# All convolution taps of x's first mixer on one engine, and the other stream's last steps moved behind the convolution

## The chip, the cores and the metric

The kernel runs on one core of a Trainium2 chip. A core has five engines with queues of their own: TensorE (PE) multiplies matrices, VectorE (DVE), ScalarE (ACT) and GpSimd (POOL) work elementwise, and SyncE (SP) issues the transfers from memory. The metric is the device time of one launch in microseconds (us). Three runs of the kernel before gave 2197.45, 2197.75 and 2201.2 us, a median of 2197.75.

## The reference

Two stacked networks run on 256 tokens of width 1024. The first (`first_block`) is a recurrent layer, an attention layer and two dense feed-forward layers. The second (`second_block`) takes its output `x` and a second stream `ctx` (here `xc`), also 256 tokens. Its layer 0 passes each stream through the same mixer, and then both streams together through a mixture of 32 experts. The change is in that mixer for `x`, and in where the last part of it for `xc` stands:

```python
def fourier_conv_mixer(h, w_in, conv_w, conv_b, conv_g, w_out):
    p = h @ w_in
    pa, pu, pg = jnp.split(p, [512, 1024], axis=-1)
    ya = jnp.fft.fft2(pa ..., axes=(1, 3), norm='ortho').real
    u = pu * jax.nn.sigmoid(pg)
    u = conv_general_dilated(u, conv_w ...) + conv_b   # depthwise, 31 taps
    yb = jax.nn.silu(rmsnorm(u, conv_g))
    return jnp.concatenate([ya, yb], axis=-1) @ w_out
...
x  = x  + g1  * fourier_conv_mixer(h, *ab)
xc = xc + cg1 * fourier_conv_mixer(hc, *ab)
...
out = hier_moe(concat([h2, hc2]), *moe)    # h2, hc2: normed x, xc
```

The convolution has 31 taps on each of 512 channels. Behind it stand a norm over the 512 channels, a SiLU, and the product with the second half of `w_out`.

## The kernel before

Features lie on the 128 partitions, tokens along the row: x and xc are 8 tiles of 128x256. A product in full precision is three products (high by high, high by low, low by high part; lines 405 to 407), so every weight chunk is first cut into a high part (ACT, line 382, `wh`) and a low part (DVE, line 383, `wl`). A chunk of 1 MB gives two such cuts, and `_K.run` makes them up to four steps ahead of the product that uses them. Products go to PSUM buffers named `mm`, of which there are three. The engine that reads a buffer out frees it for a later product.

The program is a list of steps. `_fourier` writes the mixer once for each stream. For x its steps stand in the main list: the input products (`signal`, `transform_in`), the Fourier part (`transform_rows`, `transform_cols`), the first half of the output product (`out(0, ci)`: four steps of 24 matmuls, two tiles of x each), then `gather` (what is left of the taps, and the squares), `root` (the norm's sum and inverse root), `norm` (per 128 channels a scaling on DVE, the SiLU on ACT, and the two parts), and the second half of the output product (`out(1, ci)`). Behind it come the norm and the routing of x, and the experts, whose weights (`gu`, `down`) are fetched in 1 MB pieces by SP.

For xc the steps go to a list of their own, `K.heavy`. `fill()` is called at 181 places ("spots") of the main list, and at each takes as many steps from `K.heavy` as the digit of the table HEAVY at that spot says. So HEAVY alone decides where xc's steps stand among those of x. `K.light` (the products with `mod_w`, line 1083) is spread by a second table, which does not change.

The taps are queued as closures in `K.later`, one list for DVE and one for POOL, when `signal` has made `u`. `drain` steps then take a few from each list after each product step. A tap on DVE is one instruction (line 417, `cv = u*w + cv`). A tap on POOL is an ACT product into a tile `tap` (line 421) and a POOL sum (line 424). Before the change 16 of 31 taps went to DVE into `cv` and 15 to POOL into a second sum `cg`, which `gather` adds to `cv` (line 1240). For x the three lists of interest around the end of the stage are these, by spot:

| spot | step of x behind it | steps of xc there before | steps of xc there after |
|---|---|---|---|
| 149 | signal(2), second half | out(1,0) first half | none |
| 162 to 164 | out(0, ci) | the other three halves of out(1, ci), freeing and entering of pools, the three steps of the norm before routing | none |
| 166 | root | none | all four halves of out(1, ci) |
| 167 | norm | the two scalings by that norm | pools, first step of the norm before routing |
| 168 | out(1,0) first half | router product, two turns of the tokens, a pool freed | second and third step of that norm |
| 169 | out(1,0) second half | ring of four expert buffers entered | the two scalings |
| 170, 171 | out(1,1) | none | router product and first turn; second turn and a pool freed |
| 172 | end of the mixer | none | ring of four expert buffers entered |

Of the kernel before, what the change touches and what calls it, by code (L numbers as in the profile page):

```python
# [18 lines left out]
P = 128  # L19
D = 1024  # L20
T = 256
# [132 lines left out]
class _K:  # L154
# [258 lines left out]
    def tap(self, eng, out, src, w, new, act=False):  # L413

        nc = self.nc
        if eng is nc.vector:
            eng.scalar_tensor_tensor(out, src, w, out, op0=ALU.mult, op1=ALU.add)
            return
        t = new()[:, :src.shape[1]]
        if act:  # L420
            nc.scalar.activation(t, src, AF.Copy, scale=w)
        else:
            eng.tensor_scalar(t, src, w, 0.0, op0=ALU.mult, op1=ALU.add)
        eng.tensor_tensor(out, out, t, op=ALU.add)

    def drain(self, nv=0, ng=0):

        def fn():
            for q, n in ((self.later[0], nv), (self.later[1], ng)):
                for _ in range(min(n, len(q))):  # L430
                    q.pop(0)()
        self.add(fn)
# [210 lines left out]


WARM = [8, 4, 4, 6]
HEAVY = "0000000000000100000000000000000000010101001000110000000000022001000001000000301000000010000000100001000100000000001000010000000000000000010000131301010000000000008110024100000000000"
LIGHT = "0000001101020010310001000110302000001010100100110100000500000000000000000100000000000000000100100000000000000000000000000000000000000001000011001001110000110000000001020300000000000"


# [502 lines left out]
    return ([first] if summed else [first, second, third]) + [scale(0), scale(4)]  # L1152


def _fourier(K, src, r, pool, to, conv, sums=None):

    nc = K.nc
    mm = nc.tensor.matmul
    B = _Box(K, pool)

    def begin():
        B.new("hh", [P, KC, T], F32R)
        B.new("hl", [P, KC, T], F32R)
        B.new("u", [P, 4, T + 30])
        B.new("cv", [P, 4, T])
        B._t["cg"] = B.new("cg", [P, 4, T]) if conv else B.cv
        B.new("fa", [P, 4, T])
        B.new("taps", [P, 124])
        nc.vector.tensor_scalar_mul(B.taps, K.v("conv_w_2", 0, 124), 0.5)
        nc.gpsimd.memset(B.u[:, :, 0:15], 0.0)  # L1170
        nc.gpsimd.memset(B.u[:, :, T + 15:], 0.0)

    def tap(eng, out, j, k, first):
        def fn():
            w = B.taps[:, k * 4 + j:k * 4 + j + 1]
            win = B.u[:, j, k:k + T]
            if first:
                bias = K.v("conv_b_2", j) if k == 0 else 0.0
                eng.tensor_scalar(out[:, j], win, w, bias, op0=ALU.mult, op1=ALU.add)
            else:  # L1180
                K.tap(eng, out[:, j], win, w, lambda: B.new("tap", [P, T], bufs=2), act=conv > 0)
        return fn

    def signal(j):
        def fn(h, wh, wl):
            ps = K.pt()[:, :T]
            K.lin(ps, wh, wl, B.hh, B.hl)
            if h == 0:
                B.new("sg", [P, T])

                nc.scalar.activation(B.sg, ps, AF.Tanh, scale=0.5)
            else:
                nc.vector.scalar_tensor_tensor(B.u[:, j, 15:15 + T], B.sg, 1.0, ps, op0=ALU.add, op1=ALU.mult)
                for k in range(31):
                    e = k >= conv
                    K.later[e].append(tap((nc.vector, nc.gpsimd)[e], B.cg if e else B.cv, j, k, k in (0, conv)))
        return fn

    def transform_in(ci):
        def fn(h, wh, wl):  # L1200
            ps = K.pt()[:, :T]
            K.lin(ps, wh, wl, B.hh, B.hl)
            nc.scalar.activation(B.fa[:, 2 * ci + h], ps, AF.Copy)
        return fn

    def transform_rows(g):
        def fn():
            if g == 0:
                B.new("ch", [P, KC, T], F32R, tag="hh")
                B.new("cl", [P, KC, T], F32R, tag="hl")  # L1210
            ps = K.pt()
            for t in range(2):
                mm(ps[:, t * 256:t * 256 + 256], lhsT=B.fa[:, g, t * P:t * P + P], rhs=K.dft[:, 0:256],
                   start=True, stop=True)
            B.new(f"ab{g}", [P, 2, 2, P], tag="ab", bufs=2)
            nc.scalar.activation(B._t[f"ab{g}"].rearrange("p t c j -> p (t c j)"), ps, AF.Copy)
        return fn

    def transform_cols(g):
        def fn():  # L1220
            ps = K.pt()[:, :T]
            ab = B._t[f"ab{g}"]
            for t in range(2):
                for c in range(2):
                    mm(ps, lhsT=ab[:, t, c], rhs=K.dft[:, 256 + c * 512 + t * 256:512 + c * 512 + t * 256],
                       start=t + c == 0, stop=t + c == 2)
            K.parts(B.ch[:, g], B.cl[:, g], ps)
        return fn

    rms = _Rms(K, lambda: B.cv, 4, RMS_EPS)  # L1230
    done = _Rms(K, src, KC, RMS_EPS, "acc")

    def gather():
        for q in K.later:
            while q:
                q.pop(0)()
        for q in range(2):
            if conv:
                qs = slice(2 * q, 2 * q + 2)
                nc.vector.tensor_add(B.cv[:, qs], B.cv[:, qs], B.cg[:, qs])  # L1240
            rms.square(q)

    def root():
        rms.add(0)
        rms.add(1)
        rms.root()

    def norm():
        rs = rms.row()
        for j in range(4):  # L1250
            nc.vector.scalar_tensor_tensor(B.cv[:, j], B.cv[:, j], K.v("conv_norm_g_2", j), rs,  # L1251
                                           op0=ALU.mult, op1=ALU.mult)
            nc.scalar.activation(B.cv[:, j], B.cv[:, j], AF.Silu)
            K.parts(B.ch[:, 4 + j], B.cl[:, 4 + j], B.cv[:, j])

    def out(part, ci):
        def fn(h, wh, wl):
            for i in range(2):
                m = 4 * ci + 2 * h + i
                c = slice(i * P, i * P + P)  # L1260
                ps = K.pt()[:, :T]
                K.lin3(ps, lambda k: wh[:, k, c], lambda k: wl[:, k, c], lambda k: B.ch[:, 4 * part + k],
                       lambda k: B.cl[:, 4 * part + k], 4)
                nc.vector.scalar_tensor_tensor(src[:, m], ps, K.mod[0][:, r, 16 + m:17 + m], src[:, m],
                                               op0=ALU.mult, op1=ALU.add)
            if part == 1 and conv:
                q = 2 * ci + h
                done.square(q)
                if q > 0:
                    done.add(q - 1)  # L1270
        return fn

    def drain(n=1):
        if to is None:
            K.drain(5 * n, 3 * n)

    def weights(*args, **kw):
        n = len(K.steps)
        K.addw(*args, to=to, **kw)
        if to is None:  # L1280
            last = K.steps.pop()
            drain()
            K.fill()
            K.steps.append(last)
            drain()

    K.add(begin, to)
    def here():
        if to is None:
            K.fill()  # L1290
    for fn in _modulate(K, src, 0, r, 0, K.v("norm_mix_g_2", 0, 8), pool, parts=lambda: (B.hh, B.hl), rms=sums):
        K.add(fn, to)
        here()
    for j in range(4):
        weights("w_in_ab_2", j, signal(j))
        here()
    for ci in range(2):
        weights("w_in_ab_2", 4 + ci, transform_in(ci))
        here()
    for g in range(5):  # L1300
        if g < 4:
            K.add(transform_rows(g), to)
        if g > 0:
            K.add(transform_cols(g - 1), to)
        drain()
        here()
    for ci in range(2):
        weights("w_out_ab_2", ci, out(0, ci), kind=(4, 256))
        here()
    for fn in (gather, root, norm):  # L1310
        K.add(fn, to)
        here()
    for ci in range(2):
        weights("w_out_ab_2", 2 + ci, out(1, ci), kind=(4, 256))
        here()
    if conv:
        K.add(lambda: done.add(KC // 2 - 1))
    return done

# [945 lines left out]
def _kernel(ctx, tc, a):  # L2265
    K = _K(ctx, tc, a)
# [2 lines left out]
    K.add(lambda: K.enter("big"))  # L2269
    for l in range(DEPTH):  # L2270
        _modulation(K, l, K.light)
    _fourier(K, K.xc, 1, "cx", K.heavy, 0)
    moe = _Moe(K, 0, [(K.xc, 1), (K.x, 0)])
    K.add(lambda: K.leave("cx"), K.heavy)
    K.add(moe.enter, K.heavy)
# [4 lines left out]
    sums = _first_block(K, X)  # L2280
    K.add(lambda: K.leave("big"))
    K.add(lambda: K.enter("mx"))
    rms = _fourier(K, K.x, 0, "mx", None, 16, sums)
    K.flush(K.heavy)
    K.flush(K.light)
    K.add(lambda: K.leave("mx"))
# [11 lines left out]
    sums = moe.rms  # L2298
    moe = later
    rms = _attention(K, sums)  # L2300
# [23 lines left out]
```

## Time and profile before

| | |
|---|---|
| profiled execution | 2197.75 us, of which the span is 2196.0 us |
| PE busy | 1937.6 us, 88% of the span |
| DVE busy | 1128.7 us, 51% |
| ACT busy | 812.6 us, 37% |
| POOL busy | 422.9 us, 19% |
| x's first mixer, from the first `u` to the sum of the last norm's squares | 823.25 to 958.05 us of the span |
| first expert product | 983.74 us |

The page's shares are means over the whole span, and the change touches 135 us of it. It is read from windows of the span, which give each engine's busy time and PE's granted clock in one stretch, and from the timeline, where a row is one instruction or a run of equal ones: start, time from the first's start to the last's end, engine, line, operation, output and inputs, shapes, count, and in brackets the idle time before it and what ended it. Matmuls whose operands are plain f32 are recorded as two passes each (lines 564, 1083, 1225, 1727, 1738 among them), so that their counts are twice those of the program; those of lines 405 to 407 are recorded once.

### The profile page before, as it was taken

To read this page: it belongs to the slowest core of one execution; us is meant where nothing else is said; L and a number is where in the kernel's file an instruction comes from. 1 tells how busy PE (TensorE), PEld (TensorE's weight loads), DVE (VectorE), ACT (ScalarE), POOL (GpSimd) and SP (SyncE) were. 2 spreads that over 40 slices of the span, in tenths; PEclk is the share of its full clock that TensorE was granted. 3 is DMA by queue.
4 is the path that set the end of the run, shared out by engine and by line. 5 is a ranking of instruction groups with operands and counts; after the bars stand their busy time and mean duration, and the time that the engine had idled before them with its cause. 6 is when DMAs were issued, how large, how long until landed. Compare 5 with 4: busy or idle time off the path is not lost. (4 is left out here: it accounts for less than half of the span.)

```text
span 2196.0 us, 34689 instructions
## 1 busy us (share of the span) xinstructions
PE 1937.6 (88%) x13286; PEld 1336.9 (61%) x13292; DVE 1128.7 (51%) x2081; ACT 812.6 (37%) x1430; POOL 422.9 (19%) x470
## 2 busy tenths in 40 slices
PE   6889999999979998788999898997999897787876
PEld 6769997988979977663444444434877442233332
DVE  7665673666847568753443443445554332222333
ACT  5544653554546446432222222224454221111221
POOL 5122430799952106300000000001000000000000
PEclk9999999999989999899999899998999999988998
DMA  6477655543444544368999699992224899999995
GB/s 240 175 300 267 235 214 224 219 147 142 155 152 173 192 173 173 137 267 333 419 418 419 259 396 418 419 408 77 99 77 180 323 417 418 419 418 418 419 418 218
DMA packets 86428, 602.65 MB, mean 274 GB/s; under 512 B 9632, under 2 KB 12064, under 8 KB 13856
## 3 DMA queue, kind: packets, MB, share of 16 engines
q1 hardware_dynamic: 86176, 599.24, 68.8%
q8 instruction: 164, 2.69, 0.5%
q14 instruction: 88, 0.72, 0.1%
HBM read 598.15 MB, written 1.05 MB: 273 GB/s over the span
## 5 line engine op out<-in xcount | busy, mean ns | idle before, releaser
L405 PE MATMUL mm<-xh,wh 128*128 128x256 f32 x1024 | 294.0, 287 | 12.2 <-ACT wh L382 11.4
L407 PE MATMUL mm<-xh,wl 128*128 128x256 f32 x1024 | 292.0, 285 | 5.8 <-DVE wl L383 4.8
L406 PE MATMUL mm<-xl,wh 128*128 128x256 f32 x1024 | 292.1, 285 | 0.6 <-DVE xl L480 0.3
L1972 PE MATMUL acc<-down,hT 128*64 128x512 f32 x1024 | 263.3, 623 | 7.6 <-PEq L2124 2.7
L1915 DVE TENSOR_TENSOR gs<-gs,acc 64x512 f32<-64x512 f32 x81 | 55.2, 682 | 316.4 <-ACT gs L1914 316.4
L405 PEld LDWEIGHTS mm<-xh,wh 128*128 128x128 f32 x1024 | 198.0, 193 | 21.8 <-ACT wh L382 12.3
L407 PEld LDWEIGHTS mm<-xh,wl 128*128 128x128 f32 x1024 | 197.9, 193 | 7.0 <-DVE wl L383 5.7
L406 PEld LDWEIGHTS mm<-xl,wh 128*128 128x128 f32 x1024 | 198.2, 194 | 1.8 <-DVE xl L480 1.6
L1908 PE MATMUL acc<-gu,xc 128*32 128x512 f32 x1120 | 145.1, 629 | 57.5 <-DMA gu<-in_gu_dram 47.0
L1908 PE MATMUL acc<-gu,xg 128*32 128x512 f32 x1472 | 174.3, 610 | 13.2 <-PEq L2146 6.5
L1972 PEld LDWEIGHTS acc<-down,hT 128*64 128x64 f32 x1024 | 87.8, 142 | 160.4 <-issue 143.4
L1965 DVE SCALAR_TENSOR_TENSOR yl<-acc,wsl,yh 128x512 fp32r<-128x512 f32 x64 | 48.1, 751 | 200.7 <-ACT yh L1964 186.3
L1914 ACT ACTIVATE gs<-acc 64x512 f32<-64x512 f32 x81 | 48.0, 593 | 260.7 <-PE acc L1908 259.0
L383 DVE TENSOR_TENSOR wl<-ffn_w_up,wh 128x1024 fp32r<-128x1024 f32 x96 | 126.4, 1329 | 27.0 <-ACT wh L382 26.8
L405 PE MATMUL mm<-hh,wh 128*128 128x256 f32 (+1 forms) x416 | 129.1, 310 | 6.5 <-DVE cv L1251 3.5
L1964 ACT ACTIVATE yh<-acc,wsl 128x512 fp32r<-128x512 f32 x64 | 44.0, 687 | 221.8 <-PE acc L1972 221.8
L406 PE MATMUL mm<-hl,wh 128*128 128x256 f32 (+1 forms) x416 | 124.5, 299 | 0.6 <-DVE hl L397 0.3
L407 PE MATMUL mm<-hh,wl 128*128 128x256 f32 (+1 forms) x416 | 124.0, 298 | 0.4 <-DVE wl L383 0.3
L882 DVE SCALAR_TENSOR_TENSOR hv<-mm,vec,hv 128x255 f32<-128x255 f32 x192 | 88.2, 480 | 64.1 <-ACT hv L877 60.2
L920 PE MATMUL acc<-gl,wh 128*128 128x256 f32 x384 | 109.6, 285 | 11.5 <-POOL gl L905 11.5
L1908 PEld LDWEIGHTS acc<-gu,xg 128*32 128x32 f32 x1472 | 51.3, 111 | 110.3 <-issue 88.7
L382 ACT ACTIVATE wh<-ffn_w_up 128x1024 fp32r<-128x1024 f32 x96 | 101.0, 1056 | 40.5 <-PE mm L406 17.1
(501 smaller groups left out, 4343.9 us busy)
## 6 DMA issues: line engine op xcount, KB each, us to landing
gu<-in_gu_dram SPq DMA_DIRECT2D x256, 1024.0 KB, 19.8
down<-in_down_dram SPq DMA_DIRECT2D x128, 1024.0 KB, 19.8
mod_w<-in_mod_w_dram SPq DMA_DIRECT2D x48, 1024.0 KB, 4.9
ffn_w_up<-in_ffn_w_up_dram SPq DMA_DIRECT2D x48, 1024.0 KB, 4.8
ffn_w_down<-in_ffn_w_down_dram SPq DMA_DIRECT2D x24, 1024.0 KB, 4.8
w_in_ab<-in_w_in_ab_dram SPq DMA_DIRECT2D x12, 1024.0 KB, 4.8
kv_w<-in_kv_w_dram SPq DMA_DIRECT2D x8, 1024.0 KB, 7.2
w_out_ab<-in_w_out_ab_dram SPq DMA_DIRECT2D x8, 1024.0 KB, 4.8
```

The lines of the kernel that those rows point to most:

```text
L382: nc.scalar.activation(wh, src, AF.Copy)
L383: self.lows.append(lambda: nc.vector.tensor_sub(wl, src, wh))
L405: mm(out, lhsT=wh(k), rhs=xh(k), start=s, stop=False, **kw)
L406: mm(out, lhsT=wh(k), rhs=xl(k), start=False, stop=False, **kw)
L407: mm(out, lhsT=wl(k), rhs=xh(k), start=False, stop=e, **kw)
L882: nc.vector.scalar_tensor_tensor(hv[:, s, d:], ps[:, s * T:(s + 1) * T - d], cw(2 - d, m), hv[:, s, d:], op0=ALU.mult, op1=ALU.add)
L920: mm(ps, lhsT=wh[:, k], rhs=gl[:, k], start=False, stop=False, skip_group_check=True)
L1908: mm(gu[quarters[g]], lhsT=xk(2 * j + k), rhs=w[:, k, h], start=j == 0, stop=j == 3, tile_position=(0, LOT * g), skip_group_check=True)
L1914: nc.scalar.activation(gs[to], gu[other], AF.Copy)
L1915: nc.vector.tensor_tensor(gs[to], gs[to], gu[to], op=ALU.add)
L1965: nc.vector.scalar_tensor_tensor(yl, ps, wsl, yh, op0=ALU.mult, op1=ALU.subtract)
L1972: mm(ys[n][64 * s:64 * s + 64], lhsT=hT[:, at(c)], rhs=part(ws[s], c)[:, n * 512:n * 512 + 512], start=c == 0, stop=c == 3, tile_position= ...
```

## The change

All 31 taps of x go to DVE into the one sum `cv`; the second sum, its addition and x's POOL and ACT tap instructions go. A drain takes five taps, six where it stands behind a Fourier step (`drain(6)`). `to is None` takes the place of `conv` as the sign of x. xc's taps stay on POOL. In HEAVY the last 18 steps of xc move as the table above shows.

```diff
-HEAVY = "0000000000000100000000000000000000010101001000110000000000022001000001000000301000000010000000100001000100000000001000010000000000000000010000131301010000000000008110024100000000000"
+HEAVY = "0000000000000100000000000000000000010101001000110000000000022001000001000000301000000010000000100001000100000000001000010000000000000000010000131301000000000000000000452222100000000"
...
-def _fourier(K, src, r, pool, to, conv, sums=None):
+def _fourier(K, src, r, pool, to, eng, sums=None):
...
-        B._t["cg"] = B.new("cg", [P, 4, T]) if conv else B.cv
...
-                K.tap(eng, out[:, j], win, w, lambda: B.new("tap", [P, T], bufs=2), act=conv > 0)
+                K.tap(eng, out[:, j], win, w, lambda: B.new("tap", [P, T], bufs=2))
...
                 for k in range(31):
-                    e = k >= conv
-                    K.later[e].append(tap((nc.vector, nc.gpsimd)[e], B.cg if e else B.cv, j, k, k in (0, conv)))
+                    K.later[eng is nc.gpsimd].append(tap(eng, B.cv, j, k, k == 0))
...
         for q in range(2):
-            if conv:
-                qs = slice(2 * q, 2 * q + 2)
-                nc.vector.tensor_add(B.cv[:, qs], B.cv[:, qs], B.cg[:, qs])
             rms.square(q)
...
-    def drain(n=1):
+    def drain(n=5):
         if to is None:
-            K.drain(5 * n, 3 * n)
+            K.drain(n)
...
-        drain()
+        drain(6)
...
-    _fourier(K, K.xc, 1, "cx", K.heavy, 0)
+    _fourier(K, K.xc, 1, "cx", K.heavy, K.nc.gpsimd)
...
-    rms = _fourier(K, K.x, 0, "mx", None, 16, sums)
+    rms = _fourier(K, K.x, 0, "mx", None, K.nc.vector, sums)
```

DVE's queue at the end of the taps. In the kernel before, from the last cuts ahead of `gather` to the norm: `xc<-mm` and `x<-mm` are the sums of output tiles into the streams, `cv<-cv,cg` is the addition of the two sums:

```order
L1264 SCALAR_TENSOR_TENSOR xc<-mm,mod_1090,xc 128x256 x2
L1116 SCALAR_TENSOR_TENSOR msc<-mod_1090,vec 128x8
L383 TENSOR_TENSOR wl<-w_out_ab_9630,wh 128x1024
L1264 SCALAR_TENSOR_TENSOR x<-mm,mod_1090,x 128x256 x2
L383 TENSOR_TENSOR wl<-w_out_ab_9630,wh 128x1024
L1264 SCALAR_TENSOR_TENSOR x<-mm,mod_1090,x 128x256 x2
L447 TENSOR_SCALAR ra<-mm 128x2
```

and in the changed kernel, the same place:

```order
L1259 SCALAR_TENSOR_TENSOR x<-mm,mod_1090,x 128x256 x2
L417 SCALAR_TENSOR_TENSOR cv<-u,taps,cv 128x256 x24
L383 TENSOR_TENSOR wl<-w_out_ab_9281,wh 128x1024
L1259 SCALAR_TENSOR_TENSOR xc<-mm,mod_1090,xc 128x256 x2
L383 TENSOR_TENSOR wl<-w_out_ab_9515,wh 128x1024
L1259 SCALAR_TENSOR_TENSOR xc<-mm,mod_1090,xc 128x256 x2
L383 TENSOR_TENSOR wl<-w_out_ab_9515,wh 128x1024
L1259 SCALAR_TENSOR_TENSOR xc<-mm,mod_1090,xc 128x256 x4
L447 TENSOR_SCALAR ra<-mm 128x2
```

Twenty-four taps now stand in one piece, and all eight sums of xc's tiles come behind them, ahead of the root (`ra`).

PE's queue from the sum of the convolution's squares (line 564, `mm<-sq,ones`) to the second half of x's output product. Before (`mm<-rd,ones` spreads an inverse root over the partitions, `mm<-rw,h2T` is xc's router product, `cst,h2T` its turns):

```order
L564 MATMUL mm<-sq,ones 32x256 x4
L574 MATMUL mm<-sel,tot 128x1 x2
L586 MATMUL mm<-rd,ones 128x256
L1083 MATMUL mod<-mod_w_9437,sc 32x512 x4
L1083 MATMUL mod<-mod_w_9587,sc 32x512 x4
L586 MATMUL mm<-rd,ones 128x256
L1727 MATMUL mm<-rw,h2T 128x36 x16
L1738 MATMUL acc<-cst,h2T 128x128 x12
L1738 MATMUL mm<-cst,h2T 128x128 x4
L405 MATMUL mm<-hh,wh 128x256
```

and now:

```order
L564 MATMUL mm<-sq,ones 32x256 x4
L574 MATMUL mm<-sel,tot 128x1 x2
L1083 MATMUL mod<-mod_w_9318,sc 32x512 x4
L1083 MATMUL mod<-mod_w_9439,sc 32x512 x4
L586 MATMUL mm<-rd,ones 128x256
L564 MATMUL mm<-sq,ones 32x256 x8
L574 MATMUL mm<-sel,tot 128x1 x2
L405 MATMUL mm<-hh,wh 128x256
```

The router product and the turns have left this place for the second half of the output product, and the sums of xc's norm (the second line 564 and 574) have come to stand right ahead of that half.

## Rows read from the trace of the kernel before

**Rows 1.** Windows: stretch, its length, each engine's busy time (count), PE clock, DMA.
```profile
823.00:894.00 71.00, 55.20 (x353) 44.94 (x353) 64.91 (x93) 39.90 (x77) 42.52 (x46) 0.87 0.41 149
894.00:922.00 28.00, 25.46 (x201) 22.61 (x200) 18.39 (x37) 15.31 (x27) 12.23 (x14) 0.96 0.43 153
922.00:931.00 9.00, 7.92 (x36) 3.12 (x36) 5.56 (x20) 4.29 (x10) 0.00 (x0) 0.62 0.45 157
931.00:958.00 27.00, 24.33 (x187) 19.91 (x186) 12.13 (x26) 11.06 (x22) 0.31 (x1) 0.94 0.74 293
```

**Rows 2.** Timeline, DVE, 796 to 990 us: taps, cuts, the addition.
```profile
823.25 0.42 DVE L1193 SCALAR_TENSOR_TENSOR u<-sg,mm 128x256 f32<-128x256 f32 x1
...
853.89 2.56 DVE L417 SCALAR_TENSOR_TENSOR cv<-u,taps,cv 128x256 f32<-128x256 f32 x5
856.37 1.77 DVE L383 TENSOR_TENSOR wl<-w_in_ab,wh 128x1024 fp32r<-128x1024 f32 x1
...
868.13 1.21 DVE L383 TENSOR_TENSOR wl<-w_in_ab,wh 128x1024 fp32r<-128x1024 f32 x1
...
874.16 4.42 DVE L417 SCALAR_TENSOR_TENSOR cv<-u,taps,cv 128x256 f32<-128x256 f32 x5
...
921.21 1.28 DVE L1240 TENSOR_TENSOR cv<-cv,cg 128x512 f32<-128x512 f32 x2
```

**Rows 3.** Timeline, POOL, same stretch: taps of x.
```profile
856.11 5.28 POOL L424 TENSOR_TENSOR cg<-cg,tap 128x256 f32<-128x256 f32 x5 [4.20 <-ACT tap L421]
...
873.25 10.98 POOL L424 TENSOR_TENSOR cg<-cg,tap 128x256 f32<-128x256 f32 x11 [0.94 <-ACT tap L421]
...
914.07 5.37 POOL L424 TENSOR_TENSOR cg<-cg,tap 128x256 f32<-128x256 f32 x6 [1.65 <-ACT tap L421]
```

**Rows 4.** Timeline, DVE, 796 to 990 us: from the root to the end of the norm.
```profile
925.62 0.16 DVE L447 TENSOR_SCALAR ra<-mm 128x2 f32<-128x2 f32 x1 [3.13 <-PE mm L574]
...
927.74 3.22 DVE L1149 SCALAR_TENSOR_TENSOR mt<-xc,msc,mm 128x256 f32<-128x256 f32 x8
930.92 0.48 DVE L1251 SCALAR_TENSOR_TENSOR cv<-cv,vec,mm 128x256 f32<-128x256 f32 x1
...
937.64 0.43 DVE L397 TENSOR_TENSOR hl<-cv,hh 128x256 fp32r<-128x256 f32 x1 [0.93 <-ACT hh L396]
```

**Rows 5.** Timeline, ACT, same stretch: a cut, and the squares behind the taps.
```profile
907.87 1.06 ACT L382 ACTIVATE wh<-w_out_ab 128x1024 fp32r<-128x1024 f32 x1 [0.74 <-PE mm L406]
...
921.92 1.23 ACT L551 ACTIVATE sq<-cv 128x512 f32<-128x512 f32 x2 [3.58 <-DVE cv L1240]
```

**Rows 6.** Timeline, PE, 858 to 990 us.
```profile
874.04 1.99 PE L1225 MATMUL mm<-dft,ab 128*128 128x256 f32 x8
...
892.24 3.78 PE L1225 MATMUL mm<-dft,ab 128*128 128x256 f32 x8 [4.81 <-DVE hl L397]
...
922.60 1.41 PE L564 MATMUL mm<-sq,ones 128*32 128x256 f32 x8 [1.80 <-ACT sq L551]
...
930.72 4.11 PE L1727 MATMUL mm<-rw,h2T 128*128 128x36 f32 x32
...
937.56 0.36 PE L405 MATMUL mm<-hh,wh 128*128 128x256 f32 x1
...
948.89 0.39 PE L405 MATMUL mm<-hh,wh 128*128 128x256 f32 x1
...
951.96 0.63 PE L564 MATMUL acc<-sq,ones 128*32 128x256 f32 x4
...
958.05 0.61 PE L574 MATMUL acc<-sel,tot 128*128 128x1 f32 x4 [0.48 <-ACT tot L571]
...
966.49 1.51 PE L1738 MATMUL acc<-cst,xg 128*128 128x128 f32 x12
```

**Rows 7.** Waits of SP's queue, 800 to 1010 us: us, times, longest.
```profile
SPq L315 <- PEq L2124: 45.5, 2, 32.4
```

**Rows 8.** Waits of PE, 980 to 1560 us.
```profile
PE acc L1908 <- DMA gu<-in_gu_dram: 3.9, 3, 2.7
```

More of the change, by code (lines that the diff above doesn't have):

```diff
@@ L1265, in fn @@
                                                op0=ALU.mult, op1=ALU.add)
-            if part == 1 and conv:
+            if part == 1 and to is None:
                 q = 2 * ci + h
@@ L1315, in _fourier @@
         here()
-    if conv:
+    if to is None:
         K.add(lambda: done.add(KC // 2 - 1))
```

## The prediction, made before the changed kernel ran

> **What bounds the kernel now.** I read the windows of the stage first, then the timelines of DVE, POOL, ACT and PE in it, then the waits of SP and PE behind it. From 823 to 894 us DVE works 64.9 of 71 us, while PE has 55.2 at a granted clock of 0.87 [rows 1]: here DVE sets the pace. Part of its time is contention. Five taps take 2.56 us while POOL rests, and 4.42 us beside eleven POOL sums; a cut takes 1.21 or 1.77 us [rows 2, 3]. From 894 to 922 us PE has 25.5 of 28 us of work, and the taps on POOL end last: its last run of six goes from 914.07 to 919.4, and the addition of the two sums ends at 922.5 [rows 1 to 3]. Then comes a chain in which each engine waits for the next: squares, their sum, the inverse root, and the norm, whose first instruction starts at 930.92 and whose last ends at 938.1 [rows 4, 5]. PE does not stand still in it: xc's router product and turns run from 930.72 until x's output product starts at 937.56 [rows 6]. The stage ends with the sum of the last squares at 958.05.
>
> Does a shift of that end reach the end of the kernel? Up to 1010 us SP waited 45.5 us for branches of PE, and in all of the layer's expert part PE waited only 3.9 us for a `gu` transfer [rows 7, 8]. So the buffers are full when PE comes to the experts, and what PE loses ahead of them is lost. In the changed SP queue the first five `gu` go into the main ring, as the last cuts and `mod_w` products free it, and nine more pieces follow the last turn. The first expert product needs four, and before it stood 25.7 us behind 958.05 (at 983.74). I cost the transfers at nothing; if that cover fails, they cost some microseconds on top.
>
> **Part 1, all taps on DVE.** Gone are 60 ACT products, 60 POOL instructions and the addition of 1.28 us. ACT had 39.9 us of work in 71 [rows 1], so its relief is worth nothing by itself. From 823.25, where the first `u` is made, DVE's queue up to the last tap holds: 124 taps at 0.51 us, the quiet price (2.56 / 5), 63.5 us; 14 cuts at 1.21, 16.9; xc's norm in four columns, as long as x's from 930.92 to 938.07, 7.2; four `u`, four low parts of the Fourier columns and eight sums into x, 16 instructions of 0.40 to 0.43 [rows 2, 4], 6.6. Together 94.2 us, so the last tap ends at 917.5, against 922.5 before: 5.0 us gained. The price of a tap is bounded from below by 0.40, that of instructions of the same form that don't feed each other (8 in 3.22) [rows 4], and from above by 0.88 (4.42 / 5). I take the quiet one, since it is the same instruction in the same chain and no POOL work is left in the stretch.
>
> The contended price goes with POOL's reads in rows 2 and 3. The Trainium skill ("SBUF — State Buffer", "Who interferes with whom") says that a DVE instruction with two SBUF inputs and a GpSimd instruction that reads SBUF exclude each other for a whole instruction. By that rule 0.51 stays and the sum stands; were the slow taps slow for another cause, 124 of them would cost 109 us, 46 more, and that is a rival below.
>
> **Part 2, xc's output product behind the taps.** It has eight PSUM tiles, 1.55 us each at full clock, since a step of two takes 3.07 (948.89 to 951.96) [rows 6]. PE can put down three of them while DVE works at the 24 taps in one piece, the last 12.2 us; then all three `mm` buffers wait for sums that stand behind those taps. The last two sums into x free buffers just ahead of those taps, at 905.3, so three tiles end, and PE rests, from about 908.5. What frees the first buffer is, after 917.5: the second half of the squares on ACT, 0.6, since the cut of the fourth weight half stands behind it there; that cut, 1.06; its low part on DVE, 1.21; the sum, 0.40 [rows 2, 4, 5]: 920.8. Five tiles are left. After a rest of 4.81 us PE ran eight passes in 3.78 us that took 1.99 without one [rows 6], the lower of its two clock levels (1.2 of 2.4 GHz); a tile then costs 2.9. I take two such tiles and three at 1.55, 10.5 us (all slow 14.5, all fast 7.7): 931.3. From the first product of the squares to the root 3.0 us pass at the low clock (922.60 to 925.62) and some 2.3 at the high one, with 0.7 less for the eight passes: 933.6. The root takes 2.1 (925.62 to 927.74), the product that spreads it 0.6. The norm starts at 936.3 instead of 930.92: 5.4 us later. So the 5.0 won at the taps are more than given back.
>
> The skill ("TensorE: Matmul & The Clock Gate", "HAM oscillation") warns that PE re-throttles in waits for others and starts its next burst cold. The rows of 874.04 and 892.24 agree, 1.99 against 3.78 us. With the clock kept up throughout, part 2 would come to 2.8 us less.
>
> **Part 3, xc's norm and routing among x's last steps.** Before, from the norm's start to the end 27.1 us pass (930.92 to 958.05), and x's output product starts 6.6 after the norm. Now the second half of xc's squares stands behind the norm on ACT and their products ahead of x's output product on PE: two squares, 1.2, then product, copy and sum, 1.7, so PE starts 2.9 later. It comes from a rest of 7 us: half of the first step at the low clock, 1.4. One more spreading product, 0.6. The router product, 16 matmuls of two passes, ran in 4.11 at a clock of 0.62 beside ACT (930.72); by half I set it at 2.0. The turns, 16 passes by the price of 12 in 1.51, 2.0 [rows 6]. Before, the last two lay under the norm's chain, where PE had nothing else; now they lie between x's steps, with PE as the bound. DVE's work there (root, cuts, scalings, 2.1 + 2.4 + 3.2) lies under PE's. Sum: 2.9 + 1.4 + 0.6 + 2.0 + 2.0 = 8.9. Bounds: 7.5 without the cold start; if all four steps run at half clock 16.
>
> **Sum.** 5.4 + 8.9 = 14.3 us, on the profiled execution's 2197.75 (span 2196.0 and 1.75 around it), which is also the median of the runs: 2212. With the clock up everywhere 10.1, 2208; with it down everywhere 5.4 + 4.0 + 16, 25.4, 2223. Those are the forecast's own ends.
>
> **Rivals.**
> *Taps at the independent price.* If the chain of sums costs DVE nothing and a tap takes 0.40, the 24 taps and all before end 13.6 us earlier; then PE's rest shrinks and the low clock goes in both places, 2.8 and 1.4. Sum 14.3 - 17.8 = -3.5: 2194, and by a gap a little smaller still (0.39, 8 in 3.22 without the last one's tail) -5: 2193, faster. It decides from a tap of 0.40 downwards. For it speaks only that the form can run so; against it five taps in a row at 0.51 with POOL at rest.
> *The late steps find room.* PE's waits between 931 and 958 are 2.7 us of 27 [rows 1]. If the router product, the turns and the third chain fill those, and DVE's eight sums come through between taps sooner than I count, part 3 falls to 4 and part 2 to 0: about 2200, no change that can be told. Against it: the order on each engine is fixed, and DVE's puts the sums behind the taps.
> *The slow taps stay.* 0.88 each whatever POOL does: 14.3 + 46, 2258. Rows 2 and 3 speak against it.
> *The end of the stage doesn't matter,* as transfers set the expert part: 2198. For it, the transfer engines are full for long stretches there; against it, rows 7 and 8.
>
> **How the numbers follow.** What a measurement of this kernel can tell from no change is about 0.2%, 4.4 us: 2193.4 to 2202.1. Forecast, between 2208 and 2223: 0.68. Taps at the independent price: 0.12, nearly all of it faster. Room for the late steps 0.10 and no effect of the end 0.06, both no change, with a little of the first on the slow side. Taps still slow 0.04. So faster 0.12, same 0.15, slower 0.73. The range runs from 2195 to 2223: it leaves out most of the first rival, the slow taps and the worst of the cold clock.
>
> **What would show it.** In the changed profile a batch of five taps takes about 2.6 us all through and the page has no POOL tap of x; the last tap ends near 917 us. On PE a gap of about 12 us opens after three tiles of xc, ended by a DVE sum into xc, and the clock stands near 0.5 behind it. The norm of x starts near 936 and x's output product some 9.5 us later; the last sum stands near 972, and the first expert product 25.7 us after it. It is wrong if the taps end before 910, if PE's gap behind the three tiles is under 6 us, or if router product and turns cost PE nothing.

## The result, and the profile after

The changed kernel took 2213.03 us (median of six runs, 2207.94 to 2218.01) against 2199.36 of before: a ratio of 1.0065, 95% interval 1.005 to 1.008. Predicted were 2212. So the total came out; neither of the two terms of its sum (5.4 and 8.9) did, and their errors nearly cancel, which is luck.

The profiled execution is the shortest of the six, 2207.94 us with a span of 2206.2. Windows of the kernel after, with the columns of [rows 1]; the last ones are cut where the work changes:

```profile
823.00:894.00 71.00, 57.45 (x390) 49.16 (x388) 62.66 (x123) 23.92 (x38) 0.00 (x0) 0.90 0.44 163
894.00:922.00 28.00, 13.75 (x95) 12.17 (x96) 24.18 (x48) 4.49 (x6) 0.00 (x0) 0.78 0.29 106
...
918.80:923.00 4.20, 4.20 (x19) 4.20 (x20) 2.65 (x5) 1.06 (x1) 0.00 (x0) 0.50 0.68 250
...
943.00:948.00 5.00, 5.00 (x27) 4.92 (x27) 4.44 (x13) 0.96 (x2) 0.00 (x0) 0.60 0.02 5
...
953.37:957.91 4.54, 4.54 (x27) 4.41 (x25) 0.74 (x3) 0.00 (x0) 0.00 (x0) 0.62 0.99 413
```

From 894 to 922 us PE worked 25.5 of 28 us before and works 13.75 now. DVE's timeline in the kernel after answers to [rows 2, 4]:

```profile
822.80 0.41 DVE L1192 SCALAR_TENSOR_TENSOR u<-sg,mm 128x256 f32<-128x256 f32 x1
826.87 2.57 DVE L417 SCALAR_TENSOR_TENSOR cv<-u,taps,cv 128x256 f32<-128x256 f32 x5
850.04 1.22 DVE L383 TENSOR_TENSOR wl<-w_in_ab,wh 128x1024 fp32r<-128x1024 f32 x1
...
903.02 12.46 DVE L417 SCALAR_TENSOR_TENSOR cv<-u,taps,cv 128x256 f32<-128x256 f32 x24
918.27 0.87 DVE L1259 SCALAR_TENSOR_TENSOR xc<-mm,mod,xc 128x256 f32<-128x256 f32 x2
929.87 0.16 DVE L447 TENSOR_SCALAR ra<-mm 128x2 f32<-128x2 f32 x1 [1.26 <-PE mm L574]
932.86 0.48 DVE L1246 SCALAR_TENSOR_TENSOR cv<-cv,vec,mm 128x256 f32<-128x256 f32 x1 [0.71 <-PE mm L586]
```

Five taps take the quiet price throughout, a cut 1.22 us, and POOL has no work. The last tap ends at 915.48. PE's timeline, to be read beside [rows 6]:

```profile
918.80 0.58 PE L405 MATMUL mm<-hh,wh 128*128 128x256 f32 x1 [12.92 <-DVE xc L1259]
928.01 0.64 PE L564 MATMUL mm<-sq,ones 128*32 128x256 f32 x8
...
940.05 1.59 PE L564 MATMUL mm<-sq,ones 128*32 128x256 f32 x8 [6.66 <-ACT sq L551]
943.00 0.56 PE L405 MATMUL mm<-hh,wh 128*128 128x256 f32 x1
947.72 0.60 PE L586 MATMUL mm<-rd,ones 128*128 128x256 f32 x2
952.96 0.66 PE L1090 MATMUL mod<-cst,sq 128*128 128x128 f32 x4 [1.93 <-ACT sq L1087]
957.91 0.63 PE L564 MATMUL acc<-sq,ones 128*32 128x256 f32 x4
958.47 3.76 PE L1722 MATMUL mm<-rw,h2T 128*128 128x36 f32 x32
...
972.85 0.61 PE L574 MATMUL acc<-sel,tot 128*128 128x1 f32 x4 [0.48 <-ACT tot L571]
...
999.23 3.64 PE L1903 MATMUL acc<-gu,xg 128*32 128x512 f32 x32
```

The wait of PE for `gu`, to be read beside [rows 8], over the stretch from 980 to 1580 us:

```profile
PE acc L1903 <- DMA gu<-in_gu_dram: 3.0, 4, 1.4
```

The rows show two rests: 12.92 us ahead of xc's fourth tile, and 6.66 us behind the norm, ahead of the second half of xc's squares. x's output product starts at 943.00, the last sum at 972.85, 14.8 us later than in [rows 6]. The first expert product follows at 999.23, 26.4 behind it, and PE waits 3.0 us for `gu` in the expert part, against 3.9 [rows 8]: the cover of the transfers held. In this execution the rest of the kernel wins back 5 of the 15 us (the span is 10.2 longer), for causes that were not followed; over all runs the medians lie 13.7 apart, and the ratio makes 14.3.

All experiments are compared in one table. Executions reach the first `u` of the stage between 822.8 and 828.3 us, by differences that arise long before it (831.4 in e4_pool_reads, in part by its own sums), so positions are counted from that `u`. "Sum ready" is the last tap or, with two sums, the end of their addition.

| kernel | sum ready | norm starts | last sum | norm to last sum | median us | ratio to before, 95% |
|---|---|---|---|---|---|---|
| before | 99.2 | 107.7 | 134.8 | 27.1 | 2199.36 | |
| after | 92.7 | 110.1 | 150.1 | 40.0 | 2213.03 | 1.005 to 1.008 |
| e1_taps_alone | 103.2 | 112.0 | 139.1 | 27.1 | 2201.56 | 1.001 to 1.0027 |
| e2_order_alone | 89.8 | 106.8 | 146.8 | 40.0 | 2207.63 | 1.0031 to 1.0057 |
| e3_out_early | 101.1 | 108.3 | 147.4 | 39.1 | 2212.48 | 1.0056 to 1.0082 |
| e4_pool_reads | 96.9 | 114.4 | 154.5 | 40.1 | 2222.83 | 1.0104 to 1.0136 |
| e5_two_chains | 91.6 | 100.7 | 128.1 | 27.4 | 2191.93 | 0.9958 to 0.9979 |
| e6_two_chains_late | 81.2 | 99.2 | 142.6 | 43.4 | 2205.84 | 1.0016 to 1.0041 |
| e7_clock_kept | 92.7 | 109.6 | 149.8 | 40.2 | 2213.52 | 1.0055 to 1.0082 |
| e8_scalings_later | 92.7 | 110.1 | 147.5 | 37.4 | 2211.51 | 1.0036 to 1.0066 |
| e9_squares_earlier | 92.7 | 110.6 | 147.5 | 36.9 | 2213.1 | 1.0046 to 1.0072 |
| e10_both_moves | 92.7 | 110.4 | 146.3 | 35.9 | 2208.84 | 1.0032 to 1.0058 |
| e11_taps_in_waits | 87.1 | 96.2 | 123.6 | 27.4 | 2190.15 | 0.9938 to 0.9964 |
| e12_clock_in_chain | 87.1 | 95.0 | 122.4 | 27.4 | 2184.79 | 0.992 to 0.9945 |

In every kernel but e4_pool_reads, whose first `u` comes later too, the last sum and the median (against the runs of before that were timed with it) move by the same amount within 2.2 us. So what is lost ahead of the experts is lost, as the prediction had it.

### The profile page after: what moved, and what is told of

Read it like the earlier page. It is cut to its first block, busy times and chain, and to the rows that moved or that the text cites. A ratio compares the mean times of both kernels' runs of the same rounds, so it can differ in the third digit from the quotient of the medians.

```text
span 2206.2 us, 34591 instructions
## 1 busy us (share of the span) xinstructions
PE 1930.8 (88%) x13292; PEld 1336.9 (61%) x13292; DVE 1138.0 (52%) x2139; ACT 788.9 (36%) x1374; POOL 368.6 (17%) x410
## 5 line engine op out<-in xcount | busy, mean ns | idle before, releaser
L405 PE MATMUL mm<-xh,wh 128*128 128x256 f32 x1024 | 293.1, 286 | 11.0 <-ACT wh L382 10.1
L405 PE MATMUL mm<-hh,wh 128*128 128x256 f32 (+1 forms) x416 | 130.8, 314 | 16.3 <-DVE xc L1259 12.9
L920 PE MATMUL acc<-gl,wh 128*128 128x256 f32 x384 | 109.5, 285 | 11.5 <-POOL gl L905 11.5
L1903 PEld LDWEIGHTS acc<-gu,xc 128*32 128x32 f32 x1120 | 30.9, 110 | 141.5 <-DMA gu<-in_gu_dram 86.9
```

What stands on the lines that cost most here:

```text
L405: mm(out, lhsT=wh(k), rhs=xh(k), start=s, stop=False, **kw)
L920: mm(ps, lhsT=wh[:, k], rhs=gl[:, k], start=False, stop=False, skip_group_check=True)
L1903: mm(gu[quarters[g]], lhsT=xk(2 * j + k), rhs=w[:, k, h], start=j == 0, stop=j == 3, tile_position=(0, LOT * g), skip_group_check=True)
```

## The experiments

### The two halves of the change apart

e1_taps_alone is the changed kernel with the order of before, e2_order_alone the kernel before with the changed order (HEAVY from spot 149 to 172):

```diff
-HEAVY 000000000000000004522221   (after)
+HEAVY 100000000000081100241000   (before, in e1_taps_alone)
```
```diff
-HEAVY 100000000000081100241000   (before)
+HEAVY 000000000000000004522221   (after, in e2_order_alone)
```

> All 31 taps of x on DVE as in the changed kernel, xc's last 18 steps where they stood before. My theory (the order costs, the taps gain): DVE's queue to the last tap is that of the changed kernel (915.5 us) and 8 sums into xc, 3.2, and one inverse root, 2.1, longer, so the last tap ends near 921 against 922.5 for the addition of before; from there to the end nothing changes: 1.5 us faster than before, 2196 to 2199, no change that can be told, and PE shows no gap of 12 us. Rival (the taps on DVE themselves cost, by holding up sums and cuts for PE): 2208 to 2214, as the changed kernel.

> Taps split 16 and 15 as before, xc's last 18 steps in the changed order. My theory: POOL's last taps still end near 919 and the addition near 922, 6.5 us behind the last tap of the changed kernel, and DVE's sums into xc stand behind that addition, so PE rests before its fourth tile until about 922 and everything behind is 6.5 us later than in the changed kernel: 2213 + 6.5 = 2219 (2215 to 2223). Rival (order costs nothing, the taps do): 2197 to 2201.

Both expectations missed. e1_taps_alone is slower than before, by 4.2 us (0.0019 of 2199), where I had expected no change. e2_order_alone costs 9.7 us by the ratio, 12.0 at the last sum, and not 20. DVE and then PE in e1_taps_alone:

```profile
908.77 2.56 DVE L417 SCALAR_TENSOR_TENSOR cv<-u,taps,cv 128x256 f32<-128x256 f32 x5
...
914.15 12.45 DVE L417 SCALAR_TENSOR_TENSOR cv<-u,taps,cv 128x256 f32<-128x256 f32 x24
...
935.37 0.48 DVE L1246 SCALAR_TENSOR_TENSOR cv<-cv,vec,mm 128x256 f32<-128x256 f32 x1
```
```profile
927.38 1.07 PE L564 MATMUL mm<-sq,ones 128*32 128x256 f32 x4 [13.62 <-ACT sq L551]
```

The taps end at 926.60, 4.0 later from the first `u` than the addition of before, and PE rests here too, on the convolution itself. So taps on DVE don't gain time; they lose 4. DVE's work in the stretch, before and in e1_taps_alone:

```profile
823.25:922.49 99.24, 80.41 (x551) 67.30 (x550) 83.54 (x129) 55.70 (x104) 54.75 (x60) 0.90 0.42 151
823.37:926.60 103.23, 78.57 (x555) 66.90 (x553) 92.12 (x187) 31.57 (x48) 0.00 (x0) 0.89 0.43 153
```

Its 60 taps more make some 30.7 us at 0.51, and the addition that went 1.3, but DVE is busy only 8.6 longer: by this estimate, working beside POOL had cost the rest some 21 us. The earlier end in the kernel after comes from the order, which takes eight sums, three cuts and a root out of DVE's queue ahead of the last tap: 103.2 against 92.7. The kernel with POOL's taps gains as much from it, 99.2 against 89.8. That is what my expectation for e2_order_alone overlooked; its addition was ready 9.4 us earlier, and PE rested 2.6 us instead of 12.9:

```profile
918.53 0.39 PE L405 MATMUL mm<-hh,wh 128*128 128x256 f32 x1 [2.60 <-DVE xc L1264]
```

At the last sum the one half alone costs 4.3 and the other 12.0; both in one kernel, the kernel after, cost 15.3, about their sum. The column "norm to last sum" shows where the order costs: 27.1 with the old one and 40.0 with the new one, whatever engine has the taps.

### xc's output product early, its norm and routing late

```diff
-HEAVY 000000000000000004522221   (after)
+HEAVY 100000000000030000522221
```

> The changed kernel, but xc's four half steps of the output product stand where they stood before (one ahead of x's input products' end, three among the first half of x's output product); norm and routing of xc stay late as in the changed kernel. My theory: no gap of 12 us on PE; last tap at 915.5 + 3.2 = 918.7 us, norm of x at 924 to 926 against 932.9 in the changed kernel, then the same 40 us to the last sum (965): 6 to 8 us less than the changed kernel, 2205 to 2207, still 6 above before. Rival a (the late norm and routing cost nothing, all of the loss is the gap): 2193 to 2197. Rival b (the gap is nothing, all is the tail): 2211 to 2215.

2212.48, so rival b: no gain. PE's rest did not go; it moved behind the eight tiles, to the squares, since DVE must then put down xc's sums, and make three cuts, ahead of the last taps, which end 8.4 later (101.1):

```profile
927.16 1.07 PE L564 MATMUL mm<-sq,ones 128*32 128x256 f32 x4 [13.59 <-ACT sq L551]
```

The norm starts 1.8 earlier than in the kernel after, and the tail of 39.1 stays.

### What makes a tap slow

```diff
+                    if to is None and k % 2:
+                        K.later[1].append(lambda: nc.gpsimd.tensor_tensor(B.pz[:, 0], B.pz[:, 0], B.pz[:, 1], op=ALU.add))
...
-            K.drain(n)
+            K.drain(n, 3)
```

> The changed kernel, with 60 useless POOL sums of 128x256 (two SBUF inputs, a tile of their own, nobody waits for them) issued along x's taps, three per drain and the rest behind, as many and as large as POOL's sums of before. Theory of contention: a DVE tap beside a POOL sum takes 0.88 instead of 0.51 us and a cut 1.77 instead of 1.22; POOL works about 60 us, DVE loses up to 0.42 of that, 20 to 25 us, part of it ahead of x's gather: 2225 to 2240, with runs of five taps of 4.4 us in the rows. Rival (the slow taps of before came from the ACT products or the waits between them): five taps stay at 2.56 us and the time at 2211 to 2215.

2222.83, just under the range. `pz` is a tile of its own. The sums depend on nothing outside it and ran in one piece at the start, POOL's timeline first, DVE's below:

```profile
794.72 55.29 POOL L1199 TENSOR_TENSOR pz<-pz 128x256 f32<-128x256 f32 x58
```
```profile
826.20 0.64 DVE L450 TENSOR_SCALAR ry<-rw 128x2 int32<-128x2 int32 x1
...
837.40 4.46 DVE L417 SCALAR_TENSOR_TENSOR cv<-u,taps,cv 128x256 f32<-128x256 f32 x5
...
860.30 2.56 DVE L417 SCALAR_TENSOR_TENSOR cv<-u,taps,cv 128x256 f32<-128x256 f32 x5
```

Until 850 us five taps take 4.46, at 860 they take 2.56, with no ACT product anywhere in x's taps: the price goes with POOL's sums alone. They also slowed what DVE did ahead of the first `u`: that stands 8.6 us later than in the kernel after, of which 2.7 were there before POOL began. The Trainium skill ("SBUF — State Buffer", "Who interferes with whom") lets a DVE instruction with two SBUF inputs contend with a POOL instruction that reads SBUF. The taps' rows agree; a tap then costs 0.89, close to one POOL sum (0.95). The row at 826.20 has one tensor input, a form of which that sentence does not speak. Nor do the rows show that the two exclude each other for a whole instruction, as the prediction has it: one after the other they would take 1.23 us (0.51, and 0.72 for the shortest POOL sum of before).

### The price of a tap that doesn't wait for the last one

```diff
+                    acc = B.cg if to is None and k % 2 else B.cv
+                    K.later[eng is nc.gpsimd].append(tap(eng, acc, j, k, k == 0 or acc is not B.cv and k == 1))
...
+                nc.vector.tensor_add(B.cv[:, qs], B.cv[:, qs], B.cg[:, qs])
```

e5_two_chains has this with the order of before, e6_two_chains_late with the changed one.

> All taps of x on DVE, xc's steps where they stood before (as in e1_taps_alone), but the taps of a column go in turn into two sums, cv and cg, so that no tap feeds the next one; gather adds the two (1.28 us by the rows of before). Theory (a tap costs 0.51 us because it waits for the one before it; independent ones cost 0.40, as the 8 scalings in 3.22): 124 taps save 13.6, less 1.3; the convolution is done 12.3 us earlier than in e1_taps_alone, 8 earlier than before, and the time is 2187 to 2193. Rival (0.51 is the price of the form, its shifted window and its scalar from a tile, in any order): five taps stay at 2.56 us and the time is that of e1_taps_alone and 1.3 more, 2201 to 2205.

> The changed kernel, order and all, with the two sums in turn of e5_two_chains: this is the case of the prediction's first rival, taps at the independent price. If a tap falls to 0.40, the 24 taps end some 12 us earlier, PE's gap before its fourth tile shrinks from 12.9 to about 2 us, the low clock behind it goes, and the tail of 40 us behind the norm stays: 2213 - 12.3 - 1.5 = 2199 (the prediction's rival said 2193 to 2194, with a shorter tail). If the price is the form's, 2213 to 2216.

e5_two_chains took 2191.93, within its range, and beats both kernels (0.9968). On its DVE a tap starts every 0.395 us, though each still shows 0.48:

```profile
839.38 0.48 DVE L417 SCALAR_TENSOR_TENSOR cg<-u,taps,cg 128x256 f32<-128x256 f32 x1
839.78 0.48 DVE L417 SCALAR_TENSOR_TENSOR cv<-u,taps,cv 128x256 f32<-128x256 f32 x1
840.17 0.48 DVE L417 SCALAR_TENSOR_TENSOR cg<-u,taps,cg 128x256 f32<-128x256 f32 x1
...
913.47 1.29 DVE L1241 TENSOR_TENSOR cv<-cv,cg 128x512 f32<-128x512 f32 x2
```

So 0.51 was the price of the chain, not of the form. e6_two_chains_late missed: 2205.84 instead of 2199. Its sum was ready 11.5 earlier than in the kernel after, but PE came to its rest earlier too and still waited 11.12 us, and the tail grew to 43.4. Of the 3.4 us of growth, 3.2 lie where PE's clock was down: router product, first turns and x's third half step took 10.61 us, and 7.45 in the kernel after. In the two kernels:

```profile
950.44:961.05 10.61, 10.61 (x66) 10.48 (x64) 2.14 (x5) 1.83 (x3) 0.00 (x0) 0.68 0.10 39
958.47:965.92 7.45, 7.45 (x66) 7.32 (x64) 1.99 (x5) 1.72 (x3) 0.00 (x0) 1.00 0.18 76
```

Why it fell there no run shows. The prediction's first rival had the price right, and its 2193 wrong.

### The clock in PE's rests

K.warm issues bf16 matmuls that nobody reads (line 463), here into an `acc` buffer, ahead of xc's fourth tile and ahead of its second pair of sums of squares:

```diff
+                if part == 1 and to is not None and m == 3:
+                    K.warm(50, "acc")
...
+        if which == 3 and r == 1 and l == 0:
+            K.warm(26, "acc")
```

> The changed kernel with idle matmuls (bf16, 128x512, 0.22 us each, into a PSUM buffer that nobody reads) in PE's two rests: 50 ahead of xc's fourth output tile, 11.0 of 12.9 us, and 26 ahead of the second half of xc's squares, 5.7 of 6.7 us. Theory (the low clock costs what the rows show: half of 4.2 us behind the first rest, 1.4 at the squares and the total, 1.6 in x's first half step, perhaps 1.4 in its second): 5 to 6.5 us less than the changed kernel, 2206 to 2208. Rival (PE is not what sets the pace there, DVE's sums and ACT's squares are): 2211 to 2215 in spite of a granted clock near 1.0.

2213.52, the time of the rival. But the clock stayed up in one of the two places only. PE's timeline in that kernel, and its windows over the five tiles and x's second half step:

```profile
908.48 10.74 PE L463 MATMUL acc<-cst 128*128 128x512 bf16 x49
921.33 0.39 PE L405 MATMUL mm<-hh,wh 128*128 128x256 f32 x1 [2.12 <-DVE xc L1263]
930.15 0.64 PE L564 MATMUL mm<-sq,ones 128*32 128x256 f32 x8
...
942.19 1.15 PE L564 MATMUL mm<-sq,ones 128*32 128x256 f32 x8 [0.94 <-ACT sq L551]
...
947.24 0.60 PE L586 MATMUL mm<-rd,ones 128*128 128x256 f32 x2
954.24 1.11 PE L1090 MATMUL mod<-cst,sq 128*128 128x128 f32 x4 [3.69 <-ACT sq L1087]
960.24 0.62 PE L564 MATMUL acc<-sq,ones 128*32 128x256 f32 x4
```
```profile
921.33:925.00 3.67, 3.67 (x21) 3.67 (x22) 2.97 (x5) 1.06 (x1) 0.00 (x0) 0.65 0.80 286
...
955.01:960.24 5.23, 5.23 (x27) 5.09 (x25) 0.74 (x3) 0.00 (x0) 0.00 (x0) 0.53 1.01 421
```

Behind the first row of idle matmuls PE still rested 2.12 us, and one us into the five tiles the clock fell; they took 8.82 us (921.33 to 930.15), against 9.21 in the kernel after. PE ran them without a wait, so in that stretch its clock still sets the pace. Behind the second row the clock did stay up: from xc's second squares to the end of x's first half step (24 matmuls, two tiles) 5.05 us passed, not 7.67. That step ended 3.0 earlier from the first `u`. Of these 3.0, 1.8 went in the wait for ACT, 3.69 instead of 1.93, and about 1.0 behind it, where the clock now was down over the whole second half step. That step ended only 0.2 earlier. So the run does not show that the clock costs nothing: what it gave back in one place was lost in part to another engine and in part to the clock in the next place.

### Two terms of the tail

That wait of PE is for line 1087, ACT's copy of the products with `mod_w` into a tile named `sq` (the expectations call it their square). It stands on ACT behind xc's eight scaled tiles.

```diff
-HEAVY 000000000000000004522221   (after)
+HEAVY 000000000000000004520232   (e8_scalings_later)
+HEAVY 000000000000000004612221   (e9_squares_earlier)
+HEAVY 000000000000000004610232   (e10_both_moves)
```

> The changed kernel, but xc's two scalings stand one place later, behind x's second half step of output product instead of ahead of it, router product and both turns together one place behind them. Theory from e7_clock_kept (behind the norm the chain of xc's root, scalings on DVE and ACT, and the square of the mod products behind those on ACT sets PE's pace, not PE's clock): the wait of 1.93 us at the mod products goes and the half step behind it runs at the full clock (3.1 instead of 4.5): 3 us less than the changed kernel, 2209 to 2211. Rival (PE's own work sets the pace, or the scalings only wait elsewhere, ahead of the router product): 2212 to 2215.

> The changed kernel, but the step with the second half of xc's squares stands ahead of x's norm, so that on ACT they no longer wait behind the SiLUs, and xc's sum of squares comes before x's second output half by itself. By part 3 of the prediction (2.9 us for that chain): x's output product starts 7 us behind the norm's start instead of 10.1, and xc's root and scalings come earlier too, so the gain is not given back: 3 us less than the changed kernel, 2209 to 2211. Rival (given back at the mod products' wait, as the clock was in e7_clock_kept): 2212 to 2215.

> The moves of e8_scalings_later and e9_squares_earlier together. If the two terms are separate, 6 to 6.5 us less than the changed kernel: 2206 to 2208. If both removed the same wait, 2209 to 2211; if neither was on the path, 2212 to 2215.

Singly each brings the last sum 2.5 us forward, but the medians lie 1.5 and 0 from the kernel after, inside their intervals. Together they give 4 (2208.84); the intervals still overlap. In e8_scalings_later the wait is 0.78 instead of 1.93 and the half step behind it takes 3.0, as expected, but the first expert product comes only 0.3 earlier (176.1 from the first `u`, after: 176.4): the step given back lies behind the last sum, where PE's clock was down in the products of x's routing. The same work in e8_scalings_later and in the kernel after:

```profile
987.78:993.96 6.18, 6.18 (x23) 4.67 (x24) 3.19 (x9) 0.00 (x0) 0.00 (x0) 0.50 0.66 270
987.25:991.22 3.97, 3.27 (x23) 2.33 (x23) 2.63 (x8) 0.00 (x0) 0.00 (x0) 1.00 1.02 421
```

In e9_squares_earlier x's output product starts 7.8 behind the norm instead of 10.1. Its first half step then takes 5.3 instead of 4.7, at the low clock; the second takes 3.0 instead of 4.5, and without that the gain would be 1.1, not 2.5. In e10_both_moves the first expert product comes at 172.3.

### Toward a faster version

In xc's norm DVE waited 5.1 us for ACT in e5_two_chains. e11_taps_in_waits is that kernel with eleven taps put there:

```diff
+            for _ in range(min(len(K.later[0]), (2, 5)[j == 0]) if to is not None else 0):
+                K.later[0].pop(0)()
```

> e5_two_chains, and in xc's norm eleven of x's taps are put between each scaling on DVE and the low part behind it, where DVE waited for ACT (2.27 + 3 x 0.94 us, 5.1 in all). If DVE's queue up to the last tap is what sets the end of the stage, 4 to 5 us less than e5_two_chains: 2187 to 2188, the fastest. Rival (PE or the cuts have become the bound once taps cost 0.40): 2190 to 2193.

```profile
835.28 0.48 DVE L417 SCALAR_TENSOR_TENSOR cg<-u,taps,cg 128x256 f32<-128x256 f32 x1
835.68 0.48 DVE L417 SCALAR_TENSOR_TENSOR cv<-u,taps,cv 128x256 f32<-128x256 f32 x1
836.45 0.42 DVE L397 TENSOR_TENSOR hl<-cv,hh 128x256 fp32r<-128x256 f32 x1 [0.29 <-ACT hh L396]
```

The sum is ready, and the last sum ends, 4.5 earlier than in e5_two_chains, as expected, but the median is 2190.15, only 1.8 lower (3.7 by the ratios), and the intervals overlap: shown in the rows, not in the time. e12_clock_in_chain adds to it:

```diff
     def root():
+        if to is None:
+            K.warm(26, "acc")
         rms.add(0)
```

> e11_taps_in_waits with 26 idle matmuls (5.7 of 6.9 us of rest) ahead of the sum of the convolution's squares on PE. In e7_clock_kept the clock brought nothing, since ACT and DVE set the pace behind the rest. Here PE itself stands in the chain: the eight passes take 1.67 us behind the rest and 0.64 without one, the total 1.01 against 0.61. Theory (clock counts where PE is a link of the chain): root and norm start 1.4 us earlier, and router product and turns behind are shorter, 1.4 to 2 us less than e11_taps_in_waits: 2188 to 2189. Rival (given back as in e7_clock_kept): 2190 to 2191.

```profile
903.49 5.79 PE L463 MATMUL acc<-cst 128*128 128x512 bf16 x26
910.47 1.23 PE L564 MATMUL mm<-sq,ones 128*32 128x256 f32 x8 [1.20 <-ACT sq L551]
912.25 0.61 PE L574 MATMUL mm<-sel,tot 128*128 128x1 f32 x4 [0.54 <-ACT tot L571]
```

2184.79, the fastest of all (0.9932), 5.4 below e11_taps_in_waits by the medians (4.2 by the ratios); the two intervals overlap a little. From the first `u` the profiled executions show 1.2 at the last sum and 2.7 at the first expert product. The granted clock is 1.00 from 910 to 914 us; in e11_taps_in_waits, behind the rest, it is 0.50 from 915.5 to 920. So in the rows the clock counts here; what lies beyond 2.7 no row explains, and the gain in time is not shown clear of noise.

## Why the prediction came out, point by point

**Part 1, taps.** Right in the rows: 0.51 throughout, POOL gone. The sum of 94.2 us to the last tap was 92.7, so the end came 6.5 earlier from the first `u`, not 5.0. Its reading as something "won at the taps" fails: e1_taps_alone ends 4.0 later than before, e2_order_alone 9.4 earlier. The gain is the order's.

**Part 2, xc's output product behind the taps.** The mechanism held: three tiles, a rest of 12.92 ended by a sum into xc, a low clock of 0.50 behind it (918.80 to 923.00). The size did not. The last tap came 1.5 earlier than summed, the five tiles took 9.21 instead of 10.5, and from the squares' products to the root it was 1.86 instead of 2.3. So the norm started 2.4 later than before from the first `u`, instead of 5.4.

**Part 3, the tail.** It cost 12.9 us (40.0 against 27.1), not 8.9; this is the term that was mis-sized. By the rows, from start to start: x's output product starts 10.1 behind the norm, against 6.6, which is 3.5 (predicted 2.9). Its first half step takes 4.7 instead of 3.0, 1.7 (1.4). The spreading product costs 0.5 (0.6), the router product 3.6 (2.0), the turns 1.7 (2.0). Not foreseen were the longer wait for ACT, 1.93 against 1.49, and the second half step at a clock of 0.62, 4.5 instead of 3.0. Together these make 12.9. The two errors, 3.0 too much in part 2 and 4.0 too little here, nearly cancel: the total is right by luck.

**The steps that failed** are two in part 3. The first is the router product. Its clock of 0.62 is that of the window ahead of it, 922 to 931 us; over the product itself it was 0.89, so there was no half to take off. The product before and after, on PE:

```profile
930.72:934.64 3.92, 3.92 (x34) 3.92 (x32) 2.00 (x6) 2.44 (x7) 0.00 (x0) 0.89 0.89 309
958.47:962.06 3.59, 3.59 (x34) 3.59 (x33) 0.03 (x1) 0.63 (x1) 0.00 (x0) 1.00 0.36 153
```

The second is "DVE's work there (root, cuts, scalings, 2.1 + 2.4 + 3.2) lies under PE's". Behind the norm PE waits for a chain of xc's root, DVE's scalings, ACT's sums and the copy behind them, and behind that wait it runs x's second half step at the low clock, 1.5 us more. Where xc's scalings stand later, the wait falls to 0.78, that step takes 3.0, and the last sum comes 2.5 forward (e8_scalings_later); the time of the kernel does not show it. "With the clock up everywhere 10.1, 2208" stays untested, since in e7_clock_kept the clock fell in two places. The bound of 16 for four half steps at half clock is too low by the prediction's own price: 1.35 for each of eight tiles make 10.8, which with 7.5 is 18.3.

The Trainium skill's warning that PE starts its next burst cold after a wait ("TensorE: Matmul & The Clock Gate", "HAM oscillation") holds for the two rests of the kernel after: the clock is 0.50 behind 12.92 us and behind 6.66. What it costs differs from place to place: in e7_clock_kept most of what it gave back was lost again, in e12_clock_in_chain, where PE itself is the link that all wait for, 1.2 us stayed.

**The rivals.** The first did not hold for this change, whose taps cost 0.51, but its price is real: with two sums the form runs at 0.395. "The late steps find room" and "the end of the stage doesn't matter" are refuted by the tail and by the first expert product (176.4 against 160.5 from the first `u`); "the slow taps stay" by the rows and by e4_pool_reads.

## What to carry to other kernels

Where two engines slow each other, price both sides of a split (60 sums on POOL brought the convolution only 4 us forward, as they slowed what DVE kept), and break a chain of dependent instructions into two sums before moving it to another engine, which brought more here than either. Steps that lay free in another chain's waits cost their whole time once they stand among work that an engine is bound by. And what a low clock costs is not read off one stretch: an engine made faster there comes earlier to its next wait, and can rest longer and start cold behind it. Look for the chain behind the rest first, and at the clock of every stretch that follows.

## What the runs showed of the hardware

- Dependent DVE taps (128x256, f32) start every 0.51 us, independent ones every 0.395, with 0.48 shown for each: an independent one starts before the one ahead has ended. The Trainium skill ("VectorE: DVE Perf Modes", "Two Vector instructions with no wait between them") says that a held instruction starts only when every earlier one has finished; the independent taps of e5_two_chains start before that, so these were not held.
- Beside POOL sums even instructions on 128x2 elements suffer: in the root of e4_pool_reads steps of 0.16 us took 0.59 to 0.64, in turn with undisturbed ones.
- A POOL sum of 128x256 took 0.95 us (58 in 55.29).
- Thirty-two passes of 128x36 follow the granted clock: 3.59 us from their start to the next product's at 1.00, 3.92 at 0.89 (before), 4.42 at 0.80 (e9_squares_earlier, 977.85 to 982.27 us).
